# One decode step with a retrieval mixer: sample tokens from the dense table pass to the gathered rows

## Chip, cores and metric

The kernel runs on one core of one Trainium2 chip. The metric is device time in microseconds, the median of repeated executions; three executions of the kernel before gave 4127.57, 4130.05 and 4136.44.

## What is computed

The reference is one step of a one-layer decoder over 1024 prompt tokens and 64 sample tokens, 1024 wide: a state-space branch and a windowed attention branch are merged, and a retrieval mixer (PEER) follows. The mixer is what matters here:

```python
best, pos = lax.top_k(cand, PEER_TOPK)                 # 8 heads x 16 of 16384 experts
eidx = jnp.take_along_axis(cidx, pos, axis=-1).reshape(TOKEN_BLOCK, 128)
gate = jax.nn.softmax(best, axis=-1).reshape(TOKEN_BLOCK, 128)
ue = jnp.take(u_tab, eidx, axis=0)
act = jax.nn.gelu(jnp.einsum('td,tkd->tk', xb, ue))
ve = jnp.take(v_tab, eidx, axis=0)
out = jnp.einsum('tk,tkd->td', gate * act, ve)
```

Each of the 1088 tokens picks 128 of 16384 experts; a row of `u_tab` gives an activation, and the gated activations weight rows of `v_tab`. Both tables are 16384 x 1024 floats. Then a residual is added and the result is normalised.

## The kernel before

The prompt is worked on in two halves of 512 tokens. Half 0 is projected together with the 64 sample tokens (576 columns); after that the samples travel with half 1, so that its gated units (`glu`), its output projection (`w_out`), its keys and its mixer have 576 columns. The stages of half 1, in order, are `ssm`, `attention`, `glu`, `w_out` and `peer_keys(1)`.

The mixer is done in two ways. The 512 tokens of half 0 are **gathered**: four tiles of 128 tokens. `gather_u` (L1540) fetches, for each of a tile's 128 ranks, one u row per token (128 rows of 1024 floats by one indirect DMA that POOL issues, L1553); the DVE multiplies it by the token and sums it (L1557). When a tile's 128 sums are there, `weights` (L1562) applies gelu and gate, TensorE transposes the result (L1566) and it is kept as `wT`. `gather_v` (L1573) fetches, for each token, its 128 v rows (L1589), and TensorE multiplies them by the weights, four fetches (four tokens) at a time, into the PSUM tile `va` (L1605): the DVE writes a strip of weights (L1600), then come four matmuls of the first two fetches, another strip, four matmuls of the last two. All fetched rows pass through a ring of RB = 8 buffers `row`.

The 576 tokens of half 1 go through the **dense** pass (L1417): for each of 128 groups of 128 experts, scores of all tokens (`act`, L1402: 24 matmuls for each of two 288-column parts), gelu, times a dense gate array G that `gates` (L1367) made with one-hot products (tile `oij`) in blocks of 32 tokens, and then the product with `v_tab` (`outs`, L1447), added up in `acc`. High and low halves of each number make three matmuls of each product. Some scores are made ahead (`early`, L1410), while the keys of half 1 are still being chosen, and stored in `A_scr`.

The gather runs beside everything from half 1's `ssm` on. It is a Python generator: each stage calls `tick(us)`, which advances the generator by so many fetches as a rate of `RATES` says. The name beside a rate ('u', 'v' or none) says which kind is fetched in that stage. What a fetch needs later (dot, product) is put in the list `late` and recorded a few fetches afterwards (`catch_up`, L1531). `after` (L124) keeps each of these instructions behind the last ordinary matmul. A scheduler then fixes one order for each engine, and the chip keeps to it: an engine that waits holds up all that is queued behind.

A transposed weight tile and the scores share the two PSUM buffers of `trt` (L169).

Of the kernel before, what the change touches and what calls it, by code (L numbers as in the profile page):

```python
# [28 lines left out]
AB = 7  # L29
# [35 lines left out]
class Prog:  # L65
    def __init__(self, tc, a, stop=None):
        self.tc, self.nc, self.a, self.stop = tc, tc.nc, a, stop
        self.marks = []
        self.sides, self.inside, self.last, self.want = {}, False, None, None
# [13 lines left out]
    def pace(self, name, rate, want=None):  # L83
        if name in self.sides:
            self.sides[name][1] = rate
        if name == "gather":
            self.want = want
# [183 lines left out]
    def run(self):  # L271
        tc, nc, a = self.tc, self.nc, self.a
        with ExitStack() as es:
# [14 lines left out]
            self.x2, self.xn2 = d("x2_scr", [1088, D]), d("xn2_scr", [512, D])  # L288
# [10 lines left out]
    def phases(self, es):  # L299
# [22 lines left out]
        self.pace("gather", *GO[2])  # L322
# [207 lines left out]
    def mix(self, h):  # L530
# [4 lines left out]
        with tc.tile_pool(name=f"at{h}", bufs=1) as ap:  # L535
# [7 lines left out]
            else:  # L543
                self.pace("gather", *RATES[0])
# [4 lines left out]
                self.pace("gather", *RATES[1])  # L549
            with tc.tile_pool(name=f"mx{h}", bufs=1) as mp:  # L550
# [7 lines left out]
                if h:  # L558
                    self.pace("gather", *RATES[5])
# [671 lines left out]
    def peer_keys(self, h):  # L1231
# [5 lines left out]
        self.pace(*(("gather", *RATES[6]) if h else ("ahead", FILL[1])))  # L1237
        x, (xp, g, x2) = self.xf, self.x2sb
        with ExitStack() as es:
            esj = ExitStack()  # L1240
            jk = esj.enter_context(tc.tile_pool(name=f"jk{h}", bufs=1, side="left" if h else "right"))
            for i in range(ntl):
# [4 lines left out]
                if h == 0:  # L1247
                    nc.sync.dma_start(self.xn2[r0:r0 + rows], xn)
# [6 lines left out]
            with tc.tile_pool(name=f"pk{h}", bufs=1, side="right") as kp, ExitStack() as eg:  # L1255
                self.pace(*(("gather", *RATES[2]) if h else ("ahead", FILL[2])))
# [23 lines left out]
                self.pace(*(("gather", *RATES[3]) if h else ("ahead", FILL[3])))  # L1280
# [3 lines left out]
                for i in range(ntl):  # L1284
# [6 lines left out]
                    if h:  # L1291
                        self.gates(kg, i, rows, lambda: self.early(da, x))
            if h:
                self.mark("dense")
                self.pace("gather", *RATES[4])
# [71 lines left out]
    def gates(self, kp, i, rows, between):  # L1367
# [4 lines left out]
        R = rows  # L1372
# [43 lines left out]
    def dense(self, dn, da, x):  # L1416
# [4 lines left out]
        acc = dn.tile([128, 8, 576], F32, name="acc")  # L1421

        def scores(i):
            if i >= 128:
                return
            if i in self.ahd:
                A[i] = da.tile([128, 576], F32, name="a", tag="a", bufs=AB)
# [4 lines left out]
        def weights(i):  # L1432
            if i >= 128:
                return
            if i % 4 == 0:
                G[0] = dn.tile([128, 18, 4, 32], F32, name="G", tag="G", bufs=2)
                nc.sync.dma_start(G[0], self.Gd[i // 4])
            t = A.pop(i)
            tv = t.rearrange("p (b t) -> p b t", b=18)
            v.tensor_mul(tv, tv, G[0][:, :, i % 4, :])  # L1440
            W[i] = [dn.tile([128, 576], F32R, name="W" + n, tag="W" + n, bufs=6) for n in "HL"]
            self.split(W[i][0], W[i][1], t)

        def outs(r, dq, splits=SPLITS[576]):
# [10 lines left out]
            self.tick(2.9 * len(splits))  # L1455
# [23 lines left out]
        for _ in range(2):  # L1479
            t = dn.tile([128, 18, 4, 32], F32, name="G", tag="G", bufs=2).rearrange("p b i t -> p (b i t)")  # L1480
# [3 lines left out]
        for c0, c1, tiles in ((256, 576, (2, 3, 4)), (0, 256, (0, 1))):  # L1484
# [5 lines left out]
    def dense_out(self, pool, acc, g, x3, i):  # L1490
        nc, a = self.nc, self.a
        R = 128 if i < 4 else 64
        r0 = 512 + i * 128
        x3 = x3[:R]
        nc.sync.dma_start(x3, self.x2[r0:r0 + R])
        for b in range(2):
            ps = self.mmt()
            for k in range(4):
                nc.tensor.transpose(ps[:R, k * 128:(k + 1) * 128], acc[:, b * 4 + k, i * 128:i * 128 + R], self.ident)
            nc.vector.tensor_add(x3[:, b * 512:(b + 1) * 512], x3[:, b * 512:(b + 1) * 512], ps[:R])  # L1500
        self.rms(pool, x3, g, acc[:, :, min(i, 3) * 128:min(i, 3) * 128 + 128])
        nc.sync.dma_start(a["yp"][r0:r0 + R] if i < 4 else a["ys"], x3)
# [206 lines left out]
```

## Time and profile before

| what | value |
|---|---|
| median of three executions | 4130.05 us |
| the profiled execution's own time | 4117.82 us |
| its span in the profile | 4116.1 us |
| busy: PE, DVE, ACT, POOL | 94%, 65%, 35%, 33% |
| mean granted TensorE clock | 0.973 |
| DMA: bytes moved, mean rate | 1112.94 MB, 270 GB/s |
| indirect fetches: u, v | 512, 512 |

The span is the time from the first to the last instruction that the profiler saw. All sums are made against the profiled execution (4117.82 us, of which 1.7 us lie outside the span). It was 0.3% shorter than the median. PE busy is the time in which a matmul was under way; matmuls overlap, so the duration in a row of one matmul is longer than the distance from its start to the next one's start, and it is the distance that counts for a stream of them.

### The profile page before, as it was taken

To read this page: it belongs to the slowest core of one execution; us is meant where nothing else is said; L and a number is where in the kernel's file an instruction comes from. 1 tells how busy PE (TensorE), PEld (TensorE's weight loads), DVE (VectorE), ACT (ScalarE), POOL (GpSimd) and SP (SyncE) were. 2 spreads that over 40 slices of the span, in tenths; PEclk is the share of its full clock that TensorE was granted. 3 is DMA by queue.
4 is the path that set the end of the run, shared out by engine and by line. 5 is a ranking of instruction groups with operands and counts; after the bars stand their busy time and mean duration, and the time that the engine had idled before them with its cause. 6 is when DMAs were issued, how large, how long until landed. Compare 5 with 4: busy or idle time off the path is not lost.

```text
span 4116.1 us, 74467 instructions
## 1 busy us (share of the span) xinstructions
PE 3881.9 (94%) x28935; PEld 3388.9 (82%) x28935; DVE 2681.6 (65%) x6776; ACT 1440.5 (35%) x2762; POOL 1364.0 (33%) x1236
## 2 busy tenths in 40 slices
PE   8899989899989968999999998999999999999997
PEld 8789964688878755987798898988888888898884
DVE  8627233556965868877896577666666566677554
ACT  3232234233233336212278897222222222222221
POOL 1620000000004335553311233554555555543333
PEclk9999999899999979999999999999999999999998
DMA  5575589444369789897657788899998999998988
GB/s 166 164 232 166 175 284 329 154 141 149 114 207 337 274 290 341 308 340 247 237 200 244 272 288 284 324 332 327 326 331 309 328 330 327 336 351 309 341 309 291
DMA packets 449089, 1112.94 MB, mean 270 GB/s; under 512 B 44752, under 2 KB 189520, under 8 KB 443104
## 3 DMA queue, kind: packets, MB, share of 16 engines
q1 hardware_dynamic: 301280, 571.26, 41.0%
q0 software_dynamic: 147456, 536.94, 36.1%
q8 instruction: 227, 3.72, 0.4%
q14 instruction: 126, 1.03, 0.1%
HBM read 991.77 MB, written 124.27 MB: 271 GB/s over the span
## 4 chain that ended last, share of the span: by engine, by line
PE 55%; DVE 8%; issue 2%; DMA 2%; ACT 2%; POOL 1%; SPq 0%; POOLq 0%; DVEq 0%; ACTq 0%
PE mm L77 32%; PE tr L77 18%; PE va L1605 6%; DVE row L1557 2%; DVE wL L135 1%; DMA row<-in_v_tab,eT 1%; DVE oij L1391 1%; POOL row L1589 0%; DVE sm L930 0%; DMA V<-v_scr 0%; DMA row<-in_u_tab,ei 0%; DMA Q<-Q_scr 0%; ACT wH L133 0%; DVE df L1352 0%; DVE ef L1353 0%
## 5 line engine op out<-in xcount | busy, mean ns | idle before, releaser
L1553 POOL DMA_INDIRECT row<-in_u_tab,ei x512 | 667.2, 1303 | 1035.6 <-DVE row L1557 453.2
L133 ACT CAST wH<-wraw 128x1024 fp32r<-128x1024 f32 (+1 forms) x476 | 491.8, 1035 | 1318.8 <-PE mm L77 942.2
L135 DVE TENSOR_TENSOR wL<-wraw,wH 128x1024 fp32r<-128x1024 f32 (+1 forms) x476 | 578.5, 1216 | 510.6 <-ACT wH L133 443.9
L1589 POOL DMA_INDIRECT row<-in_v_tab,eT x512 | 583.8, 1140 | 879.2 <-PE va L1605 679.6
L77 PE MATMUL tr<-x2H,wH 128*128 128x288 f32 x2048 | 620.1, 303 | 9.5 <-DVE rest L1305 4.9
L1557 DVE SCALAR_TENSOR_TENSOR row<-row,gxn 128x1024 f32<-128x1024 f32 x512 | 614.3, 1220 | 21.9 <-DMA row<-in_u_tab,ei 18.8
L77 PE MATMUL tr<-x2L,wH 128*128 128x288 f32 x2048 | 617.5, 302 | 0.0
L77 PE MATMUL tr<-x2H,wL 128*128 128x288 f32 x2048 | 615.4, 300 | 0.0
L77 PE MATMUL mm<-WH,wH 128*128 128x288 f32 (+2 forms) x2048 | 481.6, 297 | 0.9 <-issue 0.9
L77 PE MATMUL mm<-WL,wH 128*128 128x288 f32 (+2 forms) x2048 | 479.6, 296 | 0.0
L77 PE MATMUL mm<-WH,wL 128*128 128x288 f32 (+2 forms) x2048 | 475.6, 296 | 0.6 <-DVE wL L135 0.6
L77 PEld LDWEIGHTS tr<-x2H,wH 128*128 128x128 f32 x2048 | 388.3, 190 | 34.4 <-issue 21.5
L77 PEld LDWEIGHTS tr<-x2L,wH 128*128 128x128 f32 x2048 | 388.0, 189 | 20.1 <-issue 20.1
L77 PEld LDWEIGHTS tr<-x2H,wL 128*128 128x128 f32 x2048 | 388.2, 190 | 16.8 <-issue 16.8
L77 PEld LDWEIGHTS mm<-WH,wH 128*128 128x128 f32 x2048 | 340.9, 188 | 42.2 <-issue 33.0
L77 PEld LDWEIGHTS mm<-WH,wL 128*128 128x128 f32 x2048 | 339.5, 188 | 33.7 <-issue 31.9
L77 PEld LDWEIGHTS mm<-WL,wH 128*128 128x128 f32 x2048 | 341.7, 188 | 28.5 <-issue 27.7
L77 PE MATMUL mm<-xnH,wH 128*128 128x288 f32 (+1 forms) x960 | 322.9, 336 | 0.0
L1460 DVE TENSOR_TENSOR acc<-acc,mm 128x288 f32<-128x288 f32 (+2 forms) x496 | 204.9, 450 | 179.2 <-PE mm L77 157.4
L77 PE MATMUL mm<-xnL,wH 128*128 128x288 f32 (+1 forms) x960 | 319.8, 333 | 0.0
L77 PE MATMUL mm<-xnH,wL 128*128 128x288 f32 (+1 forms) x960 | 319.4, 333 | 0.0
L1605 PE MATMUL va<-row,strips 128*32 128x512 f32 x2048 | 274.7, 611 | 21.5 <-DMA row<-in_v_tab,eT 18.9
(387 smaller groups left out, 7473.6 us busy)
## 6 DMA issues: line engine op xcount, KB each, us to landing
wraw<-in_vT SPq DMA_DIRECT2D x132, 512.0 KB
wraw<-in_uT SPq DMA_DIRECT2D x128, 512.0 KB
G_scr<-Gt SPq DMA_DIRECT2D x18, 2048.0 KB
G<-G_scr SPq DMA_DIRECT2D x32, 1152.0 KB
cc<-in_kc SPq DMA_DIRECT2D x48, 512.0 KB
cc<-in_vc SPq DMA_DIRECT2D x48, 512.0 KB
wraw<-in_w_g SPq DMA_DIRECT2D x32, 512.0 KB
wraw<-in_w_qp SPq DMA_DIRECT2D x32, 512.0 KB
```

The costliest lines, as they stand in the source:

```text
L77: self.last = self.nc.tensor.matmul(out, lhsT=lhsT, rhs=rhs, **kw)
L133: nc.scalar.copy(h, raw)
L135: nc.vector.tensor_sub(l, raw, h.bitcast(F32))
L1391: v.tensor_tensor(eq, io, T[:, 0:2, t0:t0 + 4].rearrange("p a t -> p t a").unsqueeze(3).to_broadcast([128, 4, 2, 128]), op=ALU.is_equal)
L1460: v.tensor_add(o, o, ps[:, :c1 - c0])
L1553: self.after(nc.gpsimd.indirect_dma_start(out=row, out_offset=None, in_=a["u_tab"], in_offset=bass.IndirectOffsetOnAxis(ap=ei[:, k:k + 1], ...
L1557: self.after(v.scalar_tensor_tensor(row, row, 1.0, xn, op0=ALU.mult, op1=ALU.mult, accum_out=act[:, k:k + 1]))
L1589: self.after(nc.gpsimd.indirect_dma_start(out=row, out_offset=None, in_=a["v_tab"], in_offset=bass.IndirectOffsetOnAxis(ap=eT[:, tk:tk + 1 ...
L1605: self.after(nc.tensor.matmul(va[0][c:c + 32, :], lhsT=self.strips[:, s, j, 31 - t - s:63 - t - s], rhs=rows[s * 2 + j][:, b * 512:(b + 1) ...
```

## The change

Half 1's dense pass takes the 512 prompt tokens alone. The 64 sample tokens become a fifth gathered tile of 64 tokens: two ranks lie side by side on the 128 partitions (`pack_samples`, `ranks_first`), so that it takes 64 u fetches and 64 v fetches. `SPLITS[512]` is one part of 512 columns, where 576 had two of 288. The generator begins with u fetches, takes turns once the u fetches lead by `LEAD` = 160, and waits with the fifth tile until it has been chosen. In a four of v rows one strip copy serves both pairs, and the matmuls begin with the pair fetched last. The rates per stage have other values.

```diff
-RATES = ((0.9, 'u'), (1.3, 'u'), (0.6, 'v'), (0.5, 'v'), (1.149, None), (0.6, 'v'), (0.3, 'v'))
+RATES = (1.0, 1.3, 1.0, 1.0, 1.2, 1.0, 0.6)
-GO = (2, 0, (0.6, 'u'))
+GO = (2, 0, 0.7)
+LEAD = 160
...
-            self.Gd, self.Ad = d("G_scr", [32, 128, 18, 4, 32]), d("A_scr", [56, 128, 576])
+            self.Gd, self.Ad = d("G_scr", [32, 128, 16, 4, 32]), d("A_scr", [56, 128, 512])
...
-                    if h:
-                        self.gates(kg, i, rows, lambda: self.early(da, x))
+                    if h and i < 4:
+                        self.gates(kg, i, lambda: self.early(da, x))
+                    elif h:
+                        self.pack_samples()
...
+    def pack_samples(self):
+        out = []
+        for n, x in zip(("gs", "es"), self.peer[1, 4]):
+            t = self.gp.tile([128, 64], F32, name=n)
+            for kh in range(2):
+                self.nc.sync.dma_start(t[kh * 64:kh * 64 + 64], x[:64, kh * 64:kh * 64 + 64])
+            out.append(t)
+        self.peer[0, 4] = tuple(out)
...
-        t = da.tile([128, 576], F32, name="a", tag="a", bufs=AB)
-        for ps, (c0, c1) in zip(self.gemm_f(a["uT"][i], x, SPLITS[576], get=self.trt), SPLITS[576]):
+        t = da.tile([128, 512], F32, name="a", tag="a", bufs=AB)
+        for ps, (c0, c1) in zip(self.gemm_f(a["uT"][i], x, SPLITS[512], get=self.trt), SPLITS[512]):
...
-        def outs(r, dq, splits=SPLITS[576]):
+        def outs(r, dq, splits=SPLITS[512]):
...
-            self.tick(2.9 * len(splits))
+            self.tick(0.01 * sum(c1 - c0 for c0, c1 in splits))
...
-        for c0, c1, tiles in ((256, 576, (2, 3, 4)), (0, 256, (0, 1))):
+        for c0, c1, tiles in ((256, 512, (2, 3)), (0, 256, (0, 1))):
...
-        while nv < 4:
-            can = [nu < 4 and nu < nv + 3, nv < nu]
-            pick = {"u": 0, "v": 1}.get(self.want, turn // 2 % 2)
-            turn += 1
+        made = [0, 0]
+        while nv < 5:
+            can = [(0, nu) in self.peer and nu < nv + 3, nv < nu]
+            if not any(can):
+                yield RATE
+                continue
+            pick = int(made[0] - made[1] >= LEAD)
             if not can[pick]:
                 pick = 1 - pick
+            made[pick] += 1
...
-                    for s in range(2):
-                        self.after(v.tensor_copy(self.strips[:, s, :, 31], self.gw[i][:, hf * 64 + t + s:hf * 64 + 64:32]))
-                    for s in range(2):
+                    w = self.gw[i][:, hf * 64:hf * 64 + 64].rearrange("p (j t) -> p t j", j=2)[:, t:t + 2]
+                    self.after(v.tensor_copy(self.strips[:, :, :, 31], w))
+                    for s in (1, 0):
                         for b in (1, 0):
                             for j in (1, 0):
```

Three places show what the scheduler made of it. `mm<-WH` and `mm<-WL` are matmuls of `outs`, `tr<-x2H` of the scores, `va<-row` those of the v rows, `tr<-ident,act` the transpose of a tile's weights, and `mm<-ident,acc` the transposes of the finished dense output.

The first is TensorE in the dense pass, where the third tile's u sums are complete. Before:

```order
L77 MATMUL mm<-WH,wH 128x288 x2
L77 MATMUL mm<-WL,wH 128x288 x2
L77 MATMUL mm<-WH,wL 128x288 x2
L1605 MATMUL va<-row,strips 32x512 x4
L1566 MATMUL tr<-ident,act 128x128
L77 MATMUL tr<-x2H,wH 128x288
```

Now:

```order
L78 MATMUL mm<-WH,wH 128x512
L78 MATMUL mm<-WL,wH 128x512
L78 MATMUL mm<-WH,wL 128x512
L1631 MATMUL va<-row,strips 32x512 x32
L1559 MATMUL tr<-ident,act 128x128
L78 MATMUL tr<-x2H,wH 128x512
```

Where half a four of v rows stood ahead of the transpose, four whole fours now stand in a row, with no dense matmul between them.

The second is TensorE at the end of the program, from the last dense matmul on. Before:

```order
L77 MATMUL mm<-WH,wL 128x256
L1499 MATMUL mm<-ident,acc 128x128 x10
L1605 MATMUL va<-row,strips 32x512 x4
L1499 MATMUL mm<-ident,acc 128x128 x6
L1605 MATMUL va<-row,strips 32x512 x32
L1695 UNCONDITIONAL_BRANCH
```

Now:

```order
L78 MATMUL mm<-WH,wH 128x256
L78 MATMUL mm<-WL,wH 128x256
L78 MATMUL mm<-WH,wL 128x256
L1508 MATMUL mm<-ident,acc 128x128 x16
L1631 MATMUL va<-row,strips 32x512 x104
L1721 UNCONDITIONAL_BRANCH
```

Four and a half fours of v rows stood behind the last dense matmul; now thirteen do.

The third is POOL's queue of fetches at the same end. Before:

```order
L1589 DMA row<-in_v_tab,eT 128x1024 x2
L1553 DMA row<-in_u_tab,ei 128x1024 x2
L1589 DMA row<-in_v_tab,eT 128x1024 x2
L1553 DMA row<-in_u_tab,ei 128x1024
L1589 DMA row<-in_v_tab,eT 128x1024 x128
```

Now:

```order
L1615 DMA row<-in_v_tab,eT 128x1024
L1581 DMA row<-in_u_tab,ei 128x1024
L1615 DMA row<-in_v_tab,eT 128x1024
L1581 DMA row<-in_u_tab,ei 128x1024
L1615 DMA row<-in_v_tab,eT 128x1024 x159
```

The kinds take turns by one instead of by two, and 159 v fetches come after the last u fetch, where there were 128.

## Rows read from the trace of the kernel before

**Rows 1.** The page's busy times, and the queue of the indirect fetches.
```profile
PE 3881.9 (94%) x28935; PEld 3388.9 (82%) x28935; DVE 2681.6 (65%) x6776; ACT 1440.5 (35%) x2762; POOL 1364.0 (33%) x1236
...
q0 software_dynamic: 147456, 536.94, 36.1%
```

**Rows 2.** Busy time by stretch: length, engines, TensorE clock, DMA share, GB/s.
```profile
1660.00:1780.00 120.00, 116.71 (x875) 115.77 (x874) 108.86 (x182) 29.46 (x44) 70.76 (x54) 1.00 0.91 331
...
1845.00:2010.00 165.00, 161.21 (x1213) 131.16 (x1211) 127.77 (x692) 38.59 (x66) 59.49 (x54) 1.00 0.71 249
2010.00:2090.00 80.00, 74.11 (x540) 67.37 (x538) 74.38 (x376) 24.75 (x43) 22.46 (x19) 0.96 0.63 224
2090.00:2576.00 486.00, 471.68 (x3678) 445.55 (x3678) 346.56 (x642) 408.18 (x878) 134.99 (x93) 0.99 0.77 262
2576.00:3611.00 1035.00, 1024.71 (x7594) 910.26 (x7593) 665.45 (x1189) 248.77 (x362) 544.17 (x457) 1.00 0.91 328
3611.00:4075.00 464.00, 463.40 (x3443) 393.77 (x3443) 298.81 (x623) 105.37 (x130) 187.20 (x168) 1.00 0.89 323
```

**Rows 3.** Timeline of TensorE: 512-column matmuls, the first and last of 44.
```profile
1236.14 0.39 PE L77 MATMUL mm<-xnH,wL 128*128 128x512 f32 x1
...
1246.18 0.39 PE L77 MATMUL mm<-xnH,wH 128*128 128x512 f32 x1
```

**Rows 4.** The same for 288 columns: the first and last of 19.
```profile
2819.76 0.29 PE L77 MATMUL tr<-x2H,wL 128*128 128x288 f32 x1
...
2822.14 0.29 PE L77 MATMUL tr<-x2H,wL 128*128 128x288 f32 x1
```

**Rows 5.** Timeline of TensorE around half a four of v rows.
```profile
2825.71 0.42 PE L77 MATMUL mm<-WL,wH 128*128 128x288 f32 x2
2826.06 1.07 PE L1605 MATMUL va<-row,strips 128*32 128x512 f32 x8
2827.06 0.54 PE L77 MATMUL mm<-WH,wL 128*128 128x288 f32 x2
2827.43 0.42 PE L77 MATMUL mm<-WH,wH 128*128 128x288 f32 x2
```

**Rows 6.** The same where both halves of a four stood together.
```profile
3979.26 0.29 PE L77 MATMUL mm<-WH,wL 128*128 128x288 f32 x1
3979.48 1.92 PE L1605 MATMUL va<-row,strips 128*32 128x512 f32 x16
3981.34 0.53 PE L77 MATMUL mm<-WH,wL 128*128 128x288 f32 x2
3981.70 0.42 PE L77 MATMUL mm<-WH,wH 128*128 128x288 f32 x2
```

**Rows 7.** The u rows' dot on DVE (all 512): shortest, median and longest, ns.
```profile
L1557 DVE SCALAR_TENSOR_TENSOR row<-row,gxn x512: 1207/1219/1275, 1226.3 to 3770.0; 128x1024 f32<-128x1024 f32 x171
```

**Rows 8.** POOL and the v fetches: what ended its idle time; one issue in the tail.
```profile
  PE va L1605: 679.6, 145
...
4091.46 0.94 POOL L1589 DMA_INDIRECT row<-in_v_tab,eT  x1 [0.30 <-issue]
```

**Rows 9.** The chain that ended last, pieces that are a fetch's landing: start, length.
```profile
1624.10 8.05 DMA row<-in_u_tab,ei
...
3184.39 11.10 DMA row<-in_v_tab,eT
```

**Rows 10.** The highest rates of the dense pass: a stretch of 20 us.
```profile
3530.00:3550.00 20.00, 20.00 (x151) 18.00 (x150) 14.27 (x26) 5.79 (x8) 9.97 (x8) 1.00 1.01 393
```

**Rows 11.** Waits of TensorE from 1845 to 2576: total, times, longest.
```profile
PE tr L1566 <- DVE act L1564: 10.0, 1, 10.0
```

**Rows 12.** Timeline of TensorE in the tail: first and last of eight halves.
```profile
4079.03 1.07 PE L1605 MATMUL va<-row,strips 128*32 128x512 f32 x8 [1.23 <-DMA row<-in_v_tab,eT]
...
4103.13 1.94 PE L1605 MATMUL va<-row,strips 128*32 128x512 f32 x8 [3.34 <-DMA row<-in_v_tab,eT]
```

More of the change, by code (lines that the diff above doesn't have):

```diff
@@ L321, in phases @@
         self.pace("ahead", FILL[4])
-        self.pace("gather", *GO[2])
+        self.pace("gather", GO[2])
         self.mark("ssm1")
@@ L543, in mix @@
             else:
-                self.pace("gather", *RATES[0])
+                self.pace("gather", RATES[0])
                 oa = ap.tile([128, 4, 64], F32, name="oa")
@@ L558, in mix @@
                 if h:
-                    self.pace("gather", *RATES[5])
+                    self.pace("gather", RATES[5])
                 self.mark(f"wout{h}")
@@ L1236, in peer_keys @@
         es2 = ExitStack()
-        self.pace(*(("gather", *RATES[6]) if h else ("ahead", FILL[1])))
+        self.pace(*(("gather", RATES[6]) if h else ("ahead", FILL[1])))
         x, (xp, g, x2) = self.xf, self.x2sb
@@ L1255, in peer_keys @@
             with tc.tile_pool(name=f"pk{h}", bufs=1, side="right") as kp, ExitStack() as eg:
-                self.pace(*(("gather", *RATES[2]) if h else ("ahead", FILL[2])))
+                self.pace(*(("gather", RATES[2]) if h else ("ahead", FILL[2])))
                 sv = [kp.tile([128, 16, 16], F32, name=f"sv{i}") for i in range(ntl)]
@@ L1279, in peer_keys @@
                         self.early(da, x)
-                self.pace(*(("gather", *RATES[3]) if h else ("ahead", FILL[3])))
+                self.pace(*(("gather", RATES[3]) if h else ("ahead", FILL[3])))
                 eg.close()
@@ L1364, in choose, with gates @@
         self.peer[h, i] = (gf, ef)
-    def gates(self, kp, i, rows, between):
+    def pack_samples(self):
[6 more added lines that the diff above has]
+        self.peer[0, 4] = tuple(out)
+    def gates(self, kp, i, between):
         nc = self.nc
@@ L1371, in gates @@
         gf, ef = self.peer[1, i]
-        R = rows
+        R = 128
         e = kp.tile([128, 2, 128], I32, name="e", tag="e", bufs=1)[:R]
@@ L1419, in dense @@
         A, W, G = {}, {}, {}
-        acc = dn.tile([128, 8, 576], F32, name="acc")
+        acc = dn.tile([128, 8, 512], F32, name="acc")
         def scores(i):
@@ L1539, in catch_up, with ranks_first @@
                 self.wait.pop(i)[1]()
+    def ranks_first(self, x):
+        nc = self.nc
+        ps = self.trt()
+        if x.shape[1] == 128:
+            nc.tensor.transpose(ps[:, :128], x, self.ident)
+            return ps[:, :128]
+        for kh in range(2):
+            r = slice(kh * 64, kh * 64 + 64)
+            nc.tensor.matmul(ps[r, :64], lhsT=x[r], rhs=self.ident[r, r], start=True, stop=True)
+        return ps[:, :64]
     def gather_u(self, i):
@@ L1544, in gather_u @@
         gf, ef = self.peer[0, i]
+        n = 128 if i < 4 else 64
         xn = gp.tile([128, D], F32, name="gxn", tag="gxn", bufs=1)
-        nc.sync.dma_start(xn, self.xn2[i * 128:(i + 1) * 128])
-        ei = gp.tile([128, 128], I32, name="ei", tag="ei", bufs=1)
+        for r in range(0, 128, n):
+            nc.sync.dma_start(xn[r:r + n], self.xn2[i * 128:i * 128 + n])
+        ei = gp.tile([128, 128], I32, name="ei", tag="ei", bufs=1)[:, :n]
         v.tensor_copy(ei, ef)
-        act = gp.tile([128, 128], F32, name="act", tag="act", bufs=2)
-        for k in range(128):
+        act = gp.tile([128, 128], F32, name="act", tag="act", bufs=2)[:, :n]
+        for k in range(n):
             row = gp.tile([128, D], F32, name="row", tag="row", bufs=RB)
@@ L1564, in weights @@
             v.tensor_mul(act, act, gf)
[L1565 to L1568 removed]
+            ps = self.ranks_first(act)
+            self.gw[i] = gp.tile([128, 128], F32, name="wT", tag="wT", bufs=3)[:, :n]
+            v.tensor_copy(self.gw[i], ps)
         self.wait[i] = [GL, weights]
@@ L1574, in gather_v @@
         v = nc.vector
-        ps = self.trt()
-        nc.tensor.transpose(ps[:, :128], self.peer[0, i][1], self.ident)
-        eT = gp.tile([128, 128], I32, name="eT", tag="eT", bufs=2)
-        v.tensor_copy(eT, ps[:, :128])
-        for hf in range(2):
+        n = 128 if i < 4 else 64
+        eT = gp.tile([128, 128], I32, name="eT", tag="eT", bufs=2)[:, :n]
+        v.tensor_copy(eT, self.ranks_first(self.peer[0, i][1]))
+        for hf in range(n // 64):
             va = []
```

54 lines of the change are left out of this document (23 added, 31 removed).

## The prediction

> **What bounds the kernel now.** I read the page's busy times first. TensorE is busy for 94% of the span and no other engine for more than 65% [rows 1]. The view by stretch then says where that holds. From 2576 to 3611 us, the dense pass while it still makes scores, TensorE is busy for 1025 of 1035 us, and from 3611 to 4075, when all scores are made, for 463 of 464; VectorE has 36% free there [rows 2]. So the dense pass is bound by TensorE. But its DMA share is 0.91 and 0.89: the second resource is close behind. Ahead of it things are mixed. From 1845 to 2090 (keys of half 1, first choice of experts) VectorE is busy for 128 of 165 and 74 of 80 us, so that anything added to it may show. From 2090 to 2576 TensorE is busy for 472 of 486.
>
> POOL's idle time ahead of v fetches ends mostly on TensorE's v matmuls (680 us, 145 times) [rows 8]: the fetches wait for a free row buffer, not the engines for a fetch. That order of things can turn round.
>
> **Prices.** 44 matmuls of 512 columns start within 10.04 us: 233.5 ns each [rows 3]. 19 of 288 columns: 132.2 ns each [rows 4]. So two parts of 288 cost 264.4 ns where one of 512 costs 233.5: the 11% fewer columns are had nearly in full. Half a four of v rows: 1.72 us from a matmul's start to that of the fifth one after it, less four matmuls of 132 ns, 1.19 us [rows 5]. A whole four in one piece: 2.44 us less three matmuls, 2.04 us [rows 6], where two halves cost 2.38. A u row's dot: 1.22 us of VectorE [rows 7]. One fetch is 128 x 1024 floats: 536.94 MB / 1024 = 0.524 MB [rows 1], as is each piece of dense weights. POOL issues one per 0.94 + 0.30 = 1.24 us [rows 8].
>
> **The change part by part.** Counts of instructions are from the built order.
>
> *Up to 1845.* 20 u dots more come before half 1's `glu` (24 us of VectorE, bounds 0 and 24; TensorE waits there for other things too, so I take 9). In `glu` (1660 to 1780, TensorE 117 of 120 us [rows 2]) seven fours of v rows come in, 7 x 2.04 = 14 us of TensorE, and 32 dots go: I take +10, bounds 0 and 14. From 1780 to 1845 fours and dots about cancel. **+19.**
>
> *1845 to 2576.* TensorE: 2784 score matmuls of 288 become 1368 of 512, 368 to 319 us; v fours 56 halves to 33 wholes, 67 us both. The gate blocks fall from 18 to 16, one ninth of their small matmuls. So at least 49 us less. VectorE: 80 more u dots are 98 us, less about 20 for the gate blocks, on top of 128 + 74 + 347 = 549. Both engines come to some 630 to 650 of 731 us, where one alone had 707. 60 of the dots fall before 2090, 73 us where VectorE had 37 + 6 free: +30 there. Later the 49 us may come off. Bounds -49 and +30; I take the near sum of both, **-15**.
>
> *2576 to 3611.* TensorE before: 6671 x 0.1322 = 882, and 114 halves x 1.19 = 136: 1018 us. After: 3407 x 0.2335 = 796, and 57 fours x 2.04 = 116: 912. What takes part of this back stands in the new order: at the end of the third and fourth u tile, four and five fours stand in a row ahead of the transpose of that tile's weights, on which the next scores depend. Each four but the first needs rows that are fetched into buffers which the four before it frees. The landing of a fetch took 8.05 to 11.10 us where the chain shows it [rows 9]; with the four's own 2.04 us that is some 12 us a turn, 7 turns, 84 us, of which 14 are in the 912 already. A wait of this sort exists today and cost 10.0 us once [rows 11]; the stretch as a whole has 10 us of idle time. I add 65: 977. Bounds 912 (the rows come while TensorE has other work) and 1000. **-58.**
>
> The other check is DMA. 455 fetches, 71 + 72 weight pieces and 19 MB of G are 332 MB: over 977 us 340 GB/s, where the stretch now has 328 at a share of 0.91 [rows 2]. Full share would be 328 / 0.91 = 360 GB/s, 922 us, so it fits with little left. A stretch of 20 us even reached 393 [rows 10].
>
> The Trainium skill, page "DMA: Bandwidth & Descriptors", section Specifications, speaks against the change here: it gives about 358 GB/s as what HBM can feed one core. By that the stretch cannot fall below 332 / 358 = 929 us, 17 us above TensorE's sum; the trace agrees on the mean (360 extrapolated) and not on short stretches (393).
>
> *3611 to 4075.* 2832 x 0.1322 = 374 and 69 halves x 1.19 = 82 before, 456 us; 1464 x 0.2335 = 342 and 30 x 2.04 = 61 after, 403. The same 7 us of other work: 410, **-54**. DMA has 127 MB there, 310 GB/s: room.
>
> *The tail.* 41 us now, from 4075 to the end. Seven halves took 24.1 us there, 6.9 a four [rows 12]: two fours share the ring, so each waits for a landing. Thirteen fours stand there now: 12 x 6.9 = 83, plus 3 for the transposes and 11 for the last output as now, 97. Bounds: POOL alone needs 4 x 1.24 = 5.0 a four, 74 in all; 7.5 a four gives 104. **+56.**
>
> Removed and moved work without a price of its own: 64 of 576 columns go from gelu, splits and sums on ScalarE and VectorE, both with room in the dense pass [rows 2]; the small DMAs of `pack_samples` lie ahead of fetches that come several hundred us later.
>
> Sum: +19 - 15 - 58 - 54 + 56 = -52. The profiled execution (4117.8) would become 4066; its median is 0.3% higher, so I take the difference off the median: 4130 - 52 = **4078 us**, own range 4040 to 4115.
>
> **Rivals.**
>
> *The saving comes in full.* If the fours in a row cost nothing, because the u rows run ahead of TensorE on the chip, the third stretch is 912 and the sum -117: 4013 us (4030 by the page's limit above). For it: POOL waits for TensorE now, not the reverse [rows 8]. Against: no matmul stands between those fours, whatever POOL does.
>
> *DMA sets the pace.* If a share of 0.91 is what this mixture of fetches and weights can hold, the third stretch needs 332 / 328 = 1013 us, and the sum is -16: 4114. For it: TensorE was never short of data at that share, so the rows do not show whether more can be had for long. Against: single stretches of 20 us at a share of 1.0 [rows 10].
>
> *The ring of eight becomes the bound, slower than before.* Before, a four was multiplied in halves, and the first two rows were free early. Now the pair fetched last comes first, so all four stay until the last has landed, and the last fetch of a four waits for the end of the four before. In the score stretch 66 to 79 dense matmuls stand between, 15.4 to 18.4 us. Four issues take 3.7 of them, so a landing may take some 11.1 us and costs nothing below that. Landings now take 8.05 to 11.10 [rows 9]: right at the point from which it decides. Eight fetches queued at once are 4.2 MB, 12.8 us at 328 GB/s. Then each of the other 48 fours waits 1.7 us, +82: 4160 us. Against: eight are in flight only when POOL is never held up, and weights would then be short as well.
>
> *The change does not do what it says*: the built order shows the 512 columns, the lead and the whole fours, so I give this nothing.
>
> **How the numbers follow.** Forecast 0.50, full saving 0.20, DMA 0.12, ring 0.18. The predicted time is the forecast's. Leaving out about half of the full saving's and half of the ring's chance, the range is 3990 to 4165; it takes in the bounds of the second and last stretch. A measurement of this kernel can tell about 0.2%, 8 us, from no change. Faster: 0.45 of the forecast, 0.20, and 0.04 of the DMA case, 0.69. Same: 0.03 + 0.06 = 0.09. Slower: 0.18, and 0.02 each of forecast and DMA case, 0.22.
>
> **What the profile after would show.** 6144 dense matmuls of 512 columns at 233 ns from start to start. The score stretch of the dense pass at 950 to 1000 us, with two gaps of 30 to 50 us in which TensorE runs only v fours, each waiting for a fetch. The stretch without scores at about 410. A tail of 90 to 105 us after the last dense matmul. VectorE above 85% from the keys to the first choice. I am wrong if the score stretch holds many short waits of v fours for fetches all along (the ring or DMA), if the two gaps are missing (the full saving), or if the stages ahead of the dense pass grow by more than 40 us (VectorE).

## The result and the profile after

The changed kernel takes **4171.07 us** (median of five, 4161.69 to 4178.10) against 4127.57 (five, 4118.61 to 4136.44): ratio 1.0099, 95% interval 1.0080 to 1.0117. It is slower by about 1%; the prediction said 4078 and faster. The profiled execution took 4173.29 us, 1.7 of them outside its span of 4171.6, which is 55.5 longer than the span before; the medians lie 43.5 apart, so some 12 us of what follows is chance of two executions.

The page of the changed kernel, busy times and the queue of the indirect fetches, answers to [rows 1]:

```profile
PE 3730.1 (89%) x23012; PEld 2937.4 (70%) x23012; DVE 2677.2 (64%) x6528; ACT 1371.4 (33%) x2557; POOL 1456.8 (35%) x1364
...
q0 software_dynamic: 165888, 604.05, 39.8%
```

TensorE's busy time fell by 152 us and its share from 94% to 89%: the work went away, the time did not. The fetches moved 67 MB more.

Where the time went is read by stretches that begin and end at the same work in both kernels. The limits are: 1400 us, the first key matmul of half 1, the first and the last `oij` matmul, the first output matmul of the dense pass, its last score matmul, its last output matmul, the end. (The forecast had fixed limits at 1845, 2576, 3611 and 4075 us of the kernel before, a few us from these.) The view by stretch gives begin and end, length, busy us and instructions of PE, PEld, DVE, ACT and POOL, granted TensorE clock, DMA share, GB/s. Before:

```profile
1400.00:1861.30 461.30, 393.88 (x2905) 334.85 (x2903) 369.94 (x860) 166.62 (x398) 208.95 (x163) 0.93 0.89 311
1861.30:2089.70 228.40, 220.63 (x1633) 188.21 (x1633) 187.12 (x1002) 54.80 (x96) 73.03 (x66) 0.99 0.67 236
2089.70:2548.70 459.00, 454.67 (x3564) 428.77 (x3563) 328.29 (x613) 400.63 (x867) 126.46 (x86) 1.00 0.76 256
2548.70:2581.50 32.80, 22.81 (x153) 22.58 (x152) 24.07 (x40) 10.53 (x17) 12.00 (x10) 0.79 1.01 358
2581.50:3615.10 1033.60, 1023.31 (x7590) 907.86 (x7589) 661.87 (x1185) 246.36 (x358) 542.07 (x454) 1.00 0.91 328
3615.10:4074.90 459.80, 459.20 (x3412) 390.57 (x3412) 296.79 (x617) 105.09 (x129) 185.73 (x168) 1.00 0.89 323
4074.90:4116.10 41.20, 14.45 (x89) 3.29 (x86) 14.80 (x63) 4.03 (x7) 10.89 (x12) 0.69 0.74 268
```

After, the same seven:

```profile
1400.00:1910.50 510.50, 414.14 (x3020) 342.37 (x3018) 364.11 (x850) 170.00 (x399) 214.71 (x184) 0.90 0.85 304
1910.50:2178.00 267.50, 226.88 (x1421) 178.09 (x1421) 239.12 (x1055) 52.38 (x87) 142.44 (x124) 0.90 0.87 309
2178.00:2657.40 479.40, 441.44 (x2443) 351.20 (x2441) 356.33 (x698) 356.97 (x745) 186.77 (x132) 0.98 0.86 287
2657.40:2688.90 31.50, 3.68 (x17) 0.59 (x16) 5.13 (x10) 1.97 (x4) 10.63 (x10) 0.60 0.92 323
2688.90:3695.00 1006.10, 926.12 (x4325) 668.85 (x4326) 647.97 (x1031) 234.84 (x301) 510.02 (x456) 0.95 0.92 335
3695.00:4074.30 379.30, 378.63 (x1971) 274.38 (x1970) 244.84 (x411) 99.86 (x125) 140.37 (x131) 1.00 0.92 332
4074.30:4171.60 97.30, 45.95 (x224) 9.84 (x222) 15.65 (x68) 3.92 (x7) 45.27 (x47) 0.62 0.83 300
```

| stretch | forecast | measured |
|---|---|---|
| up to the first key matmul | +19 | +49.2 |
| keys, choice, gate blocks, up to the first output matmul | -15 | +58.2 |
| dense pass with scores | -58 | -27.5 |
| dense pass without scores | -54 | -80.5 |
| tail | +56 | +56.1 |
| sum | -52 | +55.5 |

The dense pass and its tail came out as forecast in sum (-52 against -56), but by luck: one of its two stretches was 30 us worse than forecast and the other 26 us better. The miss of the sum stands ahead of it: +107 where +4 was forecast.

### The profile page after: what moved, and what is told of

Its sections match the earlier page's. It is cut to its first block, busy times and chain, and to the rows that moved or that the text cites. A ratio compares the mean times of both kernels' runs of the same rounds, so it can differ in the third digit from the quotient of the medians.

```text
span 4171.6 us, 62456 instructions
## 1 busy us (share of the span) xinstructions
PE 3730.1 (89%) x23012; PEld 2937.4 (70%) x23012; DVE 2677.2 (64%) x6528; ACT 1371.4 (33%) x2557; POOL 1456.8 (35%) x1364
## 4 chain that ended last, share of the span: by engine, by line
PE 65%; DVE 12%; DMA 10%; issue 6%; ACT 4%; POOL 3%; SPq 1%; POOLq 0%; ACTq 0%; DVEq 0%
PE mm L78 41%; PE tr L78 16%; PE va L1631 5%; DMA row<-in_v_tab,eT 2%; DVE row L1585 2%; DMA row<-in_u_tab,ei 2%; POOL row L1615 1%; DVE wL L134 1%; DMA Q<-Q_scr 1%; POOL row L1581 1%; PE tr L952 1%; ACT oij L1405 1%; PE va L1114 1%; ACT wH L132 1%; DMA G_scr<-Gt 1%
## 5 line engine op out<-in xcount | busy, mean ns | idle before, releaser
L78 PE MATMUL tr<-x2H,wH 128*128 128x512 f32 x1024 | 416.8, 407 | 26.0 <-DVE rest L1306 13.9
L78 PE MATMUL mm<-WH,wH 128*128 128x512 f32 (+1 forms) x1056 | 408.8, 388 | 20.2 <-ACT WH L184 19.3
L78 PE MATMUL tr<-x2H,wL 128*128 128x512 f32 x1024 | 412.7, 403 | 0.0
L78 PE MATMUL tr<-x2L,wH 128*128 128x512 f32 x1024 | 412.7, 403 | 0.0
L78 PE MATMUL mm<-WH,wL 128*128 128x512 f32 (+1 forms) x1056 | 410.2, 389 | 2.2 <-DVE wL L134 2.2
L78 PE MATMUL mm<-WL,wH 128*128 128x512 f32 (+1 forms) x1056 | 409.5, 388 | 0.0
L1471 DVE TENSOR_TENSOR acc<-acc,mm 128x512 f32<-128x512 f32 (+1 forms) x256 | 169.7, 668 | 142.2 <-PE mm L78 141.7
L78 PEld LDWEIGHTS mm<-WH,wH 128*128 128x128 f32 x1056 | 199.4, 189 | 81.6 <-ACT WH L184 21.0
L78 PEld LDWEIGHTS tr<-x2H,wH 128*128 128x128 f32 x1024 | 196.5, 192 | 83.1 <-ACT a L1418 15.3
L78 PEld LDWEIGHTS tr<-x2H,wL 128*128 128x128 f32 x1024 | 195.8, 191 | 59.1 <-issue 11.7
```

Source lines behind the costliest of these rows:

```text
L78: self.last = self.nc.tensor.matmul(out, lhsT=lhsT, rhs=rhs, **kw)
L1471: v.tensor_add(o, o, ps[:, :c1 - c0])
```

## The experiments

All edits are to the changed kernel unless said; a line of `...` stands for code left out. Runs 1 to 6, 8 to 10 and 13 are one execution each, so differences of some 10 us between them can be chance. "Key stretch" is from the first key matmul of half 1 to the first output matmul, 778 us after and 720 before; "score stretch" is the dense pass with scores.

**1. The gather held still.**

```diff
-RATES = (1.0, 1.3, 1.0, 1.0, 1.2, 1.0, 0.6)
+RATES = (1.0, 1.3, 0.001, 0.001, 1.2, 1.0, 0.001)
```

> The changed kernel with the gather held still from the start of half 1's norm to the dense pass (its rate there 0.001), everything else the same. Read: the stretch from the first key matmul of half 1 to the first output matmul of the dense pass, 778 us in the changed kernel, 720 before. Theory V (the u rows' dots on VectorE, more of them and among the key, choice and gate work, are what made it long): at most 660. Theory C (with 512 columns TensorE's own work no longer covers the chain VectorE, ScalarE, TensorE of the gate blocks, whatever the gather does): 700 or more. The end is late in any case, some 4500 us, because the fetches that are put off stand in the tail.

**2. Short dots.**

```diff
-self.after(v.scalar_tensor_tensor(row, row, 1.0, xn, op0=ALU.mult, op1=ALU.mult,
+self.after(v.scalar_tensor_tensor(row[:, :64], row[:, :64], 1.0, xn[:, :64], op0=ALU.mult, op1=ALU.mult,
...
```

> The changed kernel with each u row's dot over 64 of the 1024 columns: a dot takes some 0.15 us instead of 1.22, but still waits for its row; leaves out 15/16 of the products with the u rows. Read: the same stretch, 778 us in the changed kernel, where some 131 dots stand. Theory V as work of VectorE: it falls by 60 us or more. Theory V as waiting (VectorE stands at a dot whose row has not landed, and all behind it waits): by under 20. Theory C: by under 20.

**3. 512 columns alone**: four gathered tiles in the order of before.

```diff
-us, ws = [self.gather_u(i) for i in range(5)], [self.gather_v(i) for i in range(5)]
+us, ws = [self.gather_u(i) for i in range(4)], [self.gather_v(i) for i in range(4)]
...
-pick = int(made[0] - made[1] >= LEAD)
+pick = {"u": 0, "v": 1}.get(self.want, turn // 2 % 2)
+turn += 1
```

(with the pairs of `RATES` and `GO` of before, the dense rate 1.2; the sample tokens' rows are copied out without their experts)

> 512 columns alone: the gather as it was before (four tiles, u first, then v, then turns of two), the dense pass with 512 columns, fours still begun with the last pair; the sample tokens' experts are left out. Read: the same stretch, 720 us before, with the same dots and v rows as before. Theory V: 660 to 695 (TensorE's 49 to 60 us come off or nearly). Theory C: 710 or more. In the dense pass my price per matmul says 1033 + 460 less some 130 us.

**4. The turns of before**, five tiles: the last three lines of run 3's edit, with the same pairs of `RATES` and `GO`.

> The changed kernel, five tiles and all, with the turns and rates of before ahead of the dense pass (u rows up to glu of half 1, then v rows alone; turns of two in the dense pass): undoes the lead of 160 alone. Read: the same stretch, 778 in the changed kernel, and the part from 1400 us to the first key matmul, 511 in the changed kernel and 461 before. Theory V: the stretch falls to 695 or less and the part ahead of it to about 465. Theory C: the stretch stays at 710 or more. The tail holds 44 fours instead of 13, 44 x 6.9 = 304 us instead of 97, so the whole is about 4171 - 130 + 207 - 31 x 2.04 = 4185 us under V.

The key stretch in these four, in this order (the view by stretch, columns as above):

```profile
1917.10:2598.20 681.10, 607.64 (x3413) 521.56 (x3412) 460.68 (x1462) 408.95 (x827) 40.86 (x33) 0.94 0.50 157
```
```profile
1904.50:2643.30 738.80, 655.81 (x3878) 519.92 (x3878) 473.75 (x1749) 410.01 (x834) 303.75 (x267) 0.95 0.91 314
```
```profile
1885.50:2600.20 714.70, 643.12 (x3774) 517.63 (x3773) 491.52 (x1548) 407.81 (x831) 172.43 (x145) 0.96 0.70 234
```
```profile
1867.30:2583.70 716.40, 643.75 (x3774) 517.85 (x3773) 491.61 (x1548) 408.17 (x831) 172.51 (x145) 0.96 0.70 233
```

Neither theory alone holds. Against V: with 512 columns and the gather of before (runs 3 and 4) the stretch takes 715 and 716 us, hardly less than the 720 of before, although TensorE has 698 - 643 = 55 us less to do; and with nearly no gather (run 1) it still takes 681, 73 of them with TensorE idle. Against C alone: the changed kernel's gather adds 778 - 716 = 62 us, and with dots of 0.22 us (0.15 was expected) 40 of the 62 go. Both are at work: 50 of the 55 us do not come off, and 62 are added. (Whole times: 4468.7, 4122.7, 4102.1 and 4300.0 us. Run 4 missed its 4185 because 44 fours and the u rows left over cost a tail of 387 us.)

**5. Three tiles of one-hot pairs.**

```diff
-eq = kp.tile([128, 4, 2, 128], F32, name="oij", tag="oij", bufs=2)
+eq = kp.tile([128, 4, 2, 128], F32, name="oij", tag="oij", bufs=3)
```

(memory: `wT` with two buffers instead of three, `sh` inside `spare`, `e` in the buffer of `T`, one buffer less for half 0's `rest`)

> The changed kernel with three tiles of one-hot pairs (oij) in the gate blocks instead of two; 4 KB for it come from the scratch of the v rows' output, the third wT and e, which now shares a buffer with T. Read: the part of the gate blocks, from the first to the last oij matmul, 479 us in the changed kernel and 459 before. Theory C (VectorE, ScalarE and TensorE wait for each other around two tiles while TensorE does a piece of scores of 5.6 us): 455 or less. If instead the dots and the v rows alone fill the part, it stays within 10 us of 479.

**9. The same third tile in the kernel before** (one buffer for `eT` in place of the one of half 0's `rest`).

> The kernel before with three tiles of one-hot pairs instead of two (memory found as in the changed kernel, and one buffer for eT). Read: its gate blocks, first to last oij matmul, 459 us, of which TensorE is busy 455. Theory C says that there TensorE's own work hid the chain: 445 to 465, nothing gained. If the two tiles bounded that part before as well, it falls by 20 us or more, and the words of lost cover are wrong.

**10. The same in run 3** (memory as in run 5).

> 512 columns alone (the gather of before, sample tokens' experts left out) with three tiles of one-hot pairs. Read: first key matmul of half 1 to first output matmul of the dense pass: 720 us before, 715 with 512 columns alone. My forecast had 49 us come off there. Theory C: with the third tile they do come off, 670 or less. If not, above 700, and something else than these tiles holds that stretch.

The gate blocks, first to last `oij` matmul, of run 5 (the changed kernel with three tiles), run 9 (before with three), run 3 (512 alone with two) and run 10 (512 alone with three):

```profile
2189.90:2581.90 392.00, 373.14 (x2172) 301.30 (x2171) 332.55 (x670) 339.40 (x722) 185.78 (x116) 0.97 0.94 314
```
```profile
2109.00:2570.30 461.30, 446.34 (x3426) 414.85 (x3425) 323.52 (x610) 376.16 (x855) 115.10 (x85) 0.99 0.75 252
```
```profile
2111.40:2571.10 459.70, 424.86 (x2343) 342.58 (x2341) 298.45 (x572) 351.39 (x739) 90.01 (x72) 0.98 0.69 228
```
```profile
2104.10:2478.30 374.20, 367.29 (x2179) 302.07 (x2178) 286.45 (x566) 336.71 (x724) 106.06 (x72) 1.00 0.83 272
```

| gate blocks, us | two tiles | three tiles |
|---|---|---|
| before, 576 columns | 459.0 | 461.3 |
| 512 columns, same gather | 459.7 | 374.2 |
| changed kernel | 479.4 | 392.0 |

This bears C out. With 576 columns TensorE is the bound (455 of 459 us busy) and a third tile is worth nothing. With 512 it is worth 86 us, and the whole of run 10 takes 4015.1 us where run 3 took 4102.1 (both without the sample tokens' experts). The waits of VectorE for TensorE at these tiles, over the gate blocks (total, times, longest): before, run 3, run 10, the changed kernel, run 5:

```profile
DVE oij L1391 <- PE mm L77: 83.8, 52, 4.4
DVE oij L1404 <- PE mm L78: 117.2, 62, 5.3
DVE oij L1404 <- PE mm L78: 22.1, 17, 2.7
DVE oij L1402 <- PE mm L78: 83.6, 42, 5.8
DVE oij L1402 <- PE mm L78: 20.6, 16, 2.2
```

The kernel before had these waits too, as many us of them as the changed kernel; there they cost nothing, because TensorE was busy meanwhile. The longest, 5.8 us, is about one piece of scores, 24 x 233.5 ns [rows 3].

Behind the blocks, up to the first output matmul, run 3 and run 10:

```profile
2571.10:2600.20 29.10, 0.00 (x0) 0.00 (x0) 10.28 (x19) 1.70 (x3) 12.44 (x10) 0.50 0.96 338
2478.30:2519.20 40.90, 38.64 (x166) 30.47 (x165) 30.37 (x49) 14.20 (x22) 17.21 (x14) 1.00 0.97 358
```

With two tiles run 3's order has all pieces of scores done by the end of the blocks, and TensorE then stands still for 29 us; with three some seven pieces are left to fill that time. So a third tile takes away two kinds of idle time of TensorE: 35 us in run 3's blocks become 7, 29 us behind them become 2; its busy time in the key stretch falls by 19 as well, for the same pieces of scores. How much of the gain is the ring's own wait and how much the order that a third tile allows was not separated. Over the whole key stretch it gives 715 - 641 = 74 us in run 10 and 778 - 715 = 63 in run 5 (4130.5 us in all), and costs 11 before (run 9, 4145.8 us). Run 6 below has run 5's memory with two tiles and takes 758 us; against it the third tile gives 43.

**6. Two buffers for `gxn`.** SP's queue waits 98 us in the score stretch at the load of a tile's rows, and weight pieces stand behind it:

```profile
SPq L1574 <- DVE row L1585: 98.4, 2, 52.3
```

```diff
-xn = gp.tile([128, D], F32, name="gxn", tag="gxn", bufs=1)
+xn = gp.tile([128, D], F32, name="gxn", tag="gxn", bufs=2)
```

(memory as in run 5)

> The changed kernel with two buffers for gxn, so that the load of the next tile's rows on SP's queue need not wait for the last dots of the tile before (memory found as in the run with three one-hot tiles). The order on TensorE is the same, with four and five v fours in a row at two borders. Read: the score stretch of the dense pass, 1006 us in the changed kernel, of which TensorE idles 99. Theory S (at the borders the weight pieces stand on SP's queue behind that load, 98 us in two waits): 930 to 955, and the whole some 60 us less. Theory R (the v fours in a row wait for buffers that the four before frees, as the prediction had it): 985 or more.

The score stretch took 998.7 us, 7 less, so S is not borne out; but one of the two waits was left (44.9 us), so that it was tested by half (4143.7 us in all, most of the gain ahead of the dense pass).

**8. Turns of four.**

```diff
-pick = int(made[0] - made[1] >= LEAD)
+pick = int(made[0] - made[1] >= LEAD or made[1] % 4 != 0)
```

> The changed kernel with turns of four u and four v fetches, where it has one and one once the lead is reached. With one and one a v fetch takes the buffer of the v fetch four before it, seven more issues of 1.24 us stand between it and the last one of its four: 9 to 10 (landing and four) + 8.7 = 18.7 us for eight fetches. In turns of four: 9 to 10 + 5 = 14.5 us. Theory Q (the ring of eight sets the pace of the gather where it lags): the two border gaps shorten, the score stretch falls from 1006 to 980 or less, and the stages before lose some of the 64 us in which VectorE stands at rows not landed. Otherwise all stretches stay within 10 us.

Score stretch 1012.4, gate blocks 484.6, whole 4188.5 us: nothing gained. Q falls in this form.

**11. Lead 64, dense rate 1.25.**

```diff
-RATES = (1.0, 1.3, 1.0, 1.0, 1.2, 1.0, 0.6)
+RATES = (1.0, 1.3, 1.0, 1.0, 1.25, 1.0, 0.6)
...
-LEAD = 160
+LEAD = 64
```

> The changed kernel with a lead of 64 instead of 160 and the dense rate 1.25 instead of 1.2: in its order no place of the dense pass has more than two fours in a row, and 3 fours instead of 13 stand in the tail. Some 520 fetches fall into the score stretch instead of 456. Theory R (the border gaps come from fours in a row that wait for each other's buffers): TensorE idles under 30 us in the score stretch instead of 99, and the stretch takes 930 to 970 us; the whole some 4060. Theory D (DMA sets the pace: 365 MB in the stretch at 360 GB/s): 1010 or more, the whole 4110 or more.

R falls, as far as standing in a row is the cause. No long row of fours is left in the pass, and TensorE waits longer, at the transposes at the tiles' ends. Its waits in that score stretch (total, times, longest):

```profile
PE tr L1559 <- DVE ei L1577: 75.4, 1, 75.4
PE tr L1559 <- DVE act L1592: 51.4, 1, 51.4
```

The stretch took 1068 us, the whole 4212.0 (ratio 1.0191, 1.0170 to 1.0211).

**13. Fewer weight bytes.**

```diff
+hl = [None]
...
-h, l = self.load_piece(a["vT"][r * 4 + dq])
+if dq % 2 == 0:
+    hl[0] = self.load_piece(a["vT"][r * 4 + dq])
+h, l = hl[0]
```

> The changed kernel, but every second piece of the dense output weights is not loaded or split and the piece before it is multiplied again: leaves out half of those weights' values, with the same matmuls and fetches. In the score stretch some 35 of 142 pieces, 18 MB of 337, go away. Theory D (the DMA's pace, 333 to 338 GB/s in every kernel with 512 columns so far, holds the score stretch, and TensorE's idle time there is the gather that has fallen behind): 319 MB / 335 = 950 us, at most 965, instead of 1006, at the same 330 to 340 GB/s. Theory Q (the ring of eight buffers or the places of the fours hold the gather): 990 or more, at a lower GB/s.

The score stretch of run 1, run 11 and run 13:

```profile
2598.20:3546.80 948.60, 905.71 (x4245) 662.43 (x4246) 627.88 (x989) 235.86 (x301) 474.72 (x418) 0.97 0.93 334
```
```profile
2741.80:3809.80 1068.00, 929.27 (x4405) 669.72 (x4406) 677.89 (x1078) 235.37 (x301) 587.75 (x499) 0.93 0.93 336
```
```profile
2689.80:3654.60 964.80, 918.88 (x4341) 665.89 (x4342) 612.66 (x1004) 197.60 (x265) 523.54 (x465) 0.97 0.92 334
```

The last two figures hardly move: 333 to 341 GB/s at a share of 0.92 or 0.93 in all sixteen kernels with 512 columns, whether the stretch takes 949 us or 1070. Taking 14 of 337 MB away took 41 us away (4078.3 us in all), as D said. Run 13 does not show D all the same. Its edit also leaves out the splits of those pieces (VectorE 613 instead of 648 us), and it changed the order: at the end of the second of the two u tiles, two fours stand in a row ahead of the transpose, not five. This string of fours in the changed kernel and in run 13, up to the transpose:

```profile
3404.22 1.92 PE L1631 MATMUL va<-row,strips 128*32 128x512 f32 x16
3415.88 3.64 PE L1631 MATMUL va<-row,strips 128*32 128x512 f32 x16 [9.74 <-DVE row L1585]
3428.36 3.49 PE L1631 MATMUL va<-row,strips 128*32 128x512 f32 x16 [8.84 <-DVE row L1585]
3440.98 3.64 PE L1631 MATMUL va<-row,strips 128*32 128x512 f32 x16 [9.12 <-DMA row<-in_v_tab,eT]
3453.46 3.64 PE L1631 MATMUL va<-row,strips 128*32 128x512 f32 x16 [8.84 <-DVE row L1585]
3459.77 0.47 PE L1559 MATMUL tr<-ident,act 128*128 128x128 f32 x1 [2.68 <-DVE act L1592]
```
```profile
3397.61 1.92 PE L1634 MATMUL va<-row,strips 128*32 128x512 f32 x16 [0.77 <-DVE acc L1474]
3412.73 3.25 PE L1634 MATMUL va<-row,strips 128*32 128x512 f32 x16 [13.19 <-DVE row L1588]
3418.51 0.33 PE L1562 MATMUL tr<-ident,act 128*128 128x128 f32 x1 [2.53 <-DVE act L1595]
```

The two strings take 49.7 and 55.6 us in the changed kernel, 41.9 and 20.9 in run 13: 42 us less, as much as the whole gain. And between its two strings the changed kernel's TensorE is busy for 502 of 503 us, at a DMA share of 0.93; in them it is busy for a quarter to three tenths of the time. First string, the time between, second string:

```profile
2851.20:2900.90 49.70, 12.63 (x65) 2.57 (x66) 21.98 (x40) 0.65 (x2) 33.64 (x28) 0.64 0.86 307
2900.90:3404.20 503.30, 502.32 (x2354) 371.43 (x2354) 335.95 (x525) 129.91 (x166) 250.82 (x224) 1.00 0.93 340
3404.20:3459.80 55.60, 16.38 (x82) 3.18 (x82) 24.05 (x44) 1.24 (x2) 34.30 (x33) 0.62 0.91 328
```

Nor is the rate a ceiling. Run 16 held more for 200 us:

```profile
3120.00:3320.00 200.00, 164.51 (x758) 104.50 (x757) 124.77 (x217) 35.38 (x45) 124.71 (x111) 0.87 0.97 369
```

So the two gaps are the gather that is late at the transposes. What holds its pace there (28 and 33 instructions of POOL in the two strings, about 1.7 us each), the DMAs, the ring of eight or POOL, is not shown.

**7. Halves again.**

```diff
-self.after(v.tensor_copy(self.strips[:, :, :, 31], w))
-for s in (1, 0):
+for s in range(2):
+    self.after(v.tensor_copy(self.strips[:, s, :, 31], self.gw[i][:, hf * 64 + t + s:hf * 64 + 64:32]))
+for s in range(2):
...
```

> The changed kernel with each four multiplied in two halves again, the pair fetched first at its head, and two strip copies: undoes that part of the change alone. By my prices (2.38 against 2.04 us a four) 94 fours where TensorE is the bound would cost 32 us more, and 13 fours in the tail 13 x (6.9 - 7.5) = 8 us less: 4190 to 4200. If the buffers that come free late cost more than the shorter four saves, 4160 or less. Same within 10 us: neither matters.

4161.8 us, ratio 1.0074 (1.0058 to 1.0091) where the changed kernel has 1.0099 (1.0080 to 1.0117): no dearer, and perhaps 10 us cheaper. The price per four was about right where TensorE is the bound: without scores 388.1 us against 379.3, 0.29 us for each of 30 fours (0.34 by the prices). The tail gives it back, 84.2 against 97.3. The one strip copy and the start with the last pair are together worth nothing here.

**12, 14, 15, 16. Versions meant to beat both.** Run 12 is run 11 with three tiles and halves. Run 14 is runs 5 and 7 together, lead 160. Runs 15 and 16 have three tiles, halves and the turns rule of run 4, with these rates:

```diff
+RATES = ((1.0, 'u'), (1.3, 'u'), (1.0, 'v'), (1.0, 'v'), (1.2, None), (1.0, 'v'), (0.6, 'v'))
+RATES = ((1.0, 'u'), (1.3, 'u'), (1.0, None), (1.0, None), (1.2, None), (1.0, None), (0.6, None))
```

> A version meant to beat both: lead 64 and dense rate 1.25, three tiles of one-hot pairs, fours in halves as before. Theories C and R together: some 63 us less than the changed kernel from the tiles, 60 from the border gaps, 60 from the tail, 10 from the halves: 3980 to 4040. If DMA sets the pace of the dense pass: 4070 to 4110.

4183.4 us (ratio 1.0126): above even its dearer case. The score stretch took 1070 us at 333 GB/s, with 492 fetches.

> A version meant to beat both: the changed kernel with three tiles of one-hot pairs and the fours in halves as before, lead 160. From 4171: 41 us less as with the tiles alone, 10 less as with the halves alone: 4110 to 4130.

4102.9 us, ratio 0.9931 (0.9910 to 0.9951): better than hoped.

> The same with the turns of before (u rows up to half 1's glu, then v rows alone up to the dense pass, turns of two there) at the changed kernel's higher rates, so that as many fetches as in the changed kernel, 517 against 519, stand ahead of the dense pass, but 256 of them v rows and 261 u rows instead of 180 and 339. Theory V (u dots among keys and choice hold VectorE): the stretch from the first key matmul to the dense pass falls from 715 (three tiles) to 660 to 690, the part ahead of it by some 10 us, and the whole to 4060 to 4100. If the place of the dots does not matter: 4110 to 4130.

4112.3 us (0.9952, 0.9936 to 0.9968), not 4060 to 4100. The key stretch takes 774 us against run 14's 718, with 59 fours in it instead of 33 and 88 dots instead of 266: the fours cost more than the dots did. So what the gather costs there is not the dots' place alone. The part ahead of it fell by 31 us.

> Three tiles of one-hot pairs and halves, with u rows alone up to the end of half 1's glu (no v fours where TensorE is the bound), then turns of two all the way, at the changed kernel's rates; 500 fetches ahead of the dense pass instead of 519. If the v fours in glu are what cost the part up to the first key matmul, it falls from 1909 us (with lead 160) to 1880 or less, the stretch from there to the dense pass stays at 718 to 735, and the whole is 4075 to 4095. If the number of fetches alone counts: 4100 to 4125.

4088.0 us, ratio 0.9918 (0.9899 to 0.9938): the best. The part from 1400 us to the first key matmul takes 473 us against run 14's 509, the key stretch 707: with no v fours in `glu`, 36 us are back.

## Why the prediction was wrong

**Up to the first key matmul: mis-sized.** Forecast +19, measured +49. From `glu`'s first matmul to that of the output projection it takes 153.5 us, 139.2 before: +14, the bare price of its seven fours (7 x 2.04), where I had taken +10. The 20 u dots ahead of `glu`, taken at 9 us, go with +25. In nine kernels with the changed order and lead 160 that part takes 269 to 284 us from 1400, in seven with u rows first 244 to 266; so some 20 of the 25 is the order, and the profiled execution of before was the shortest of all. The output projection and the norm, put at nothing, took 88.4 us instead of 78.5, +10; why was not tried. With the order of before (run 4) the stretch is 467, +6.

**1845 to 2576: the step that failed.** "Bounds -49 and +30; I take the near sum of both, -15." Measured +58, outside both bounds. Two things were wrong. First, that TensorE's 49 us come off at all. I added VectorE's and TensorE's busy times and found room, but a stretch in which TensorE is busy for 455 of 459 us also hides how the other engines wait for each other: VectorE's 83.8 us of waits at the one-hot tiles were there before the change, at no cost. With less to do on TensorE they showed, and 512 columns alone gave 720 - 715 = 5 us: of the 55 us that TensorE had less to do, it stood idle for 50 more. With a third tile they gave 80. Second, I let the dots fill VectorE's free time. In the keys VectorE went from 187 of 228 us to 239 of 268, and TensorE waits there for `rest` (22.9 us in seven waits, against 4.9 in one before). The row of the waits of TensorE in the keys and first choice of the changed kernel:

```profile
PE tr L78 <- DVE rest L1306: 22.9, 7, 7.2
```

The added gather cost 62 us (run 4), 42 of them in the keys and the first choice (267.5 us against 225.4), with 16 fours there in both kernels. The dots' work is 40 of the 62 (run 2). Five more fours in the stretch, 33 instead of 28, are 10 us by their price; what the rest is was not separated.

The stages ahead of the dense pass grew by 107 us, VectorE was busy for 89% of the keys and the first choice, and the prediction had named such a growth as a sign of being wrong. It put it down to VectorE; the dots' work on VectorE is 40 of the 107.

**The dense pass with scores: mis-sized.** Forecast 977 us, measured 1006. The term that was too small is "I add 65", for the two strings of fours that wait for rows. The two gaps came at the places I named, and between them TensorE is the bound (502 of 503 us). From the first four of a string to the transpose 49.7 and 55.6 us pass, 105 in all; nine fours at 2.04 are 18 of that, so 87 stand where I had 65. The seven turns took 91 us, 84 by my 12 each, and 14 more pass between the last four of a string and the transpose, where my sum had the two fours' own time, 4. The other 7 us are in the rest of the stretch.

What the prediction did not see is that the string is only the form of the wait: with the fours spread (run 11) the gap moved to the transposes, the next thing that needs the gather, and grew to 127 us.

The rival "DMA sets the pace" gave 1013 for this stretch and came nearest in number; it had 0.12. Its mean rate held in all sixteen kernels with 512 columns, but it does not fit the 503 us in which TensorE was the bound at a share of 0.93, and no run tells it from the strings of fours. The rival of the ring, 1.7 us for each of 48 fours all along, did not come true: in the same 503 us nearly no four waits, and turns of four (run 8) gained nothing. That its 4160 us lies near the 4171 measured is chance.

The Trainium skill, page "DMA: Bandwidth & Descriptors", section Specifications, gives about 358 GB/s for one core from HBM. The mean over the stretch stayed below it in every kernel here (335 in the changed one), and 200 us of run 16 went above it (369).

**The dense pass without scores: mis-sized, to the good.** -81 instead of -54: 379 us where I had 410. Of its 1463 matmuls 192 are the last row of pieces, which has 256 columns at 0.118 us, not 0.2335 (22 us), and the other 1271 started 0.229 us apart (6 us).

**The tail: right.** 97 us, as forecast. Its first and its second-last four, with the wait before them:

```profile
4079.90 3.50 PE L1631 MATMUL va<-row,strips 128*32 128x512 f32 x16 [3.90 <-DMA row<-in_v_tab,eT]
...
4150.26 3.64 PE L1631 MATMUL va<-row,strips 128*32 128x512 f32 x16 [3.28 <-DMA row<-in_v_tab,eT]
```

They are 11 fours and 70.4 us apart, 6.4 a four, a little less than the 6.9 read from [rows 12].

In all, the change trades TensorE's time for fetches: dense pass and tail together moved from 1535 us at 325 GB/s to 1483 at 332 with as many fetches (632 and 633); the other 128 fetches went ahead of it, where the stretches grew by 107 us.

## What to carry to other kernels

Taking work from the bounding engine pays only down to what that work hid; before forecasting it, look at the waits that the other engines have now, at no cost, ask which ring of buffers ties them to the bounding engine, and whether one more buffer lets them run ahead. When a gather falls behind, the wait shows wherever the next result of it is needed, so spreading its consumers only moves the gap. A rate that is the same in sixteen runs is not yet a bound: look whether the bounding engine stands still while it holds, and whether a run that moves fewer bytes has kept its order of instructions.

## What was not expected of the hardware

The mean DMA rate of the score stretch stayed within 333 to 341 GB/s over sixteen programs that differ in turns, lead, buffers and tiles, although twenty microseconds before had shown 393 [rows 10] and 200 us of run 16 moved 369. In the dense pass output matmuls of 512 columns started 0.229 us apart and score matmuls 0.232 to 0.235, against 0.2335 in [rows 3]. In the two strings of fours, in which TensorE stood still most of the time, the granted clock was 0.64 and 0.62 of full speed, 2.4 GHz, where the lower level, 1.2 GHz, would be 0.5; over the score stretch it was 0.95, against 1.00 before.
